# The first modulation sums on quarters of the PSUM rows, and a fixed TensorE order at the start of a DeltaNet/gMLP block

## The chip, the cores and the metric

The kernel runs on one core of a Trainium2 chip. The metric is the time of one execution on the device, in microseconds (us), as the median of several runs. A core has a matrix engine (TensorE, PE in the rows; PEld are its weight loads), VectorE (DVE), ScalarE (ACT), GpSimd (POOL) and a sync engine (SP) that issues nearly all DMA transfers here. Each engine takes its own instructions strictly in order and waits where an operand is not there yet.

## The reference

One step of a hybrid backbone, one layer, over 128 context rows and 2048 latent rows of width 1024:

- modulation: `m = silu(cond) @ w_mod + b_mod` for two conditioning vectors (context and latent), six vectors of 1024 each: shift, scale and gate for the mixer and for the MLP
- `h = rmsnorm(x, norm_mix) * (1 + scale1) + shift1`
- one combined projection of `h`: query, key and value (a centred convolution of width 3 and silu follow), a gate, 16 columns for decay and beta ("ab"), and the two inputs of a spatial gating unit
- a gated DeltaNet scan in both directions, 4 heads of 128, and the spatial gating, then one output projection, residual
- the second modulated rmsnorm, a squared-ReLU MLP of width 4096, residual, final rmsnorm

The change touches only the start: the first four half-vectors of the modulation (`shift1` and `scale1`, each in two halves of 512), and the normalised, modulated and projected first block of rows.

## The kernel before

Everything is float32. A product of full precision is three matmuls of rounded parts: each operand is split into a high part (`H`, rounded) and a low part (`L`, the rest), and `mm3` (L220, L221, L222) adds H x H, L x H and H x L in one PSUM bank. A weight tile of 128x512 is split by `split_w`: ScalarE rounds (L191), VectorE subtracts (L192).

The 17 row tiles of 128 go in blocks of three; block 0 holds the context tile and two latent tiles. For a block, `column(k)` makes one of eight column tiles: for block 0 TensorE transposes the three normalised row tiles (L482) into a bank `pt`, ScalarE applies scale and shift per partition (L484, `full`), VectorE makes `kH` (L487) and `kL` (L488). `feature_tile` computes one head of key (gi 1), query (gi 0) or value (gi 2): per column tile one `mm3` with N = 388, eight in all, then `convolve` (ScalarE L534, VectorE L537, L541). Its bank comes from `pj` (three buffers), for the key head 2 of block 0 from `pt` (three buffers). `ab_block` multiplies the 16 ab columns (L609, L610; bank `pm`, two buffers).

The first modulation vectors are made on TensorE directly in float32: `mod_load` fetches eight 128x512 tiles of `w_mod`, and `mod_columns` multiplies them by the conditioning (`scond`, 128x2 per tile, L335) into the rows 0 and 1 of a `pm` bank, copies the 2x512 result (L337, `mrow`) and transposes it to columns (L340); VectorE adds the bias (L343) and, for the scale, multiplies by the norm weight (L347). This is done four times: `m0` (shift, first half), `m1` (scale, first half), `m2` and `m3` (second halves). Column tiles 0 to 3 need the first halves only, 4 to 7 the second. Ten halo rows `xh` (neighbours of the blocks for the convolution) are normalised and modulated apart (`hal`, L387 to L411).

The later modulation vectors come out of `mods`, a list of steps that the loop over heads spreads over its slots: `MOD_STEPS[n]` steps with head tile n of block 0. The first eight (`split_mod_steps`, L359, L360) run on TensorE, the others on VectorE. The order on each engine is made by a scheduler with a timeline of its own from the order of the code; the kernel's code can add ordering constraints. `wp` is a pool of 49 buffers of 128x512 in which weights and their parts rotate.

Of the kernel before, what the change touches and what calls it, by code (L numbers as in the profile page):

```python
# [18 lines left out]
P = 128  # L19
D = 1024  # L20
# [21 lines left out]
MOD_STEPS = (1, 1, 0, 0, 0, 1, 0, 2, 0, 1, 1, 2)  # L42
# [13 lines left out]
AHEAD = 3  # L56
COMPUTE = (mybir.EngineType.DVE, mybir.EngineType.Activation, mybir.EngineType.Pool)
# [5 lines left out]
def hybrid_step(  # L63
# [62 lines left out]
    def make_masks():  # L126
# [3 lines left out]
        bd = {}  # L130
        for w in (2, 4, 8, 16, 32, 64):
# [7 lines left out]
            bd[w] = m  # L139
        for w in (2, 4, 8, 16, 32):  # L140
            V.tensor_tensor(out=om[w], in0=bd[2 * w], in1=bd[w], op=ALU.subtract)
# [45 lines left out]
    def split_w(raw, pool=None, tag="w"):  # L187

        h = (pool or wp).tile([P, 512], F32R, tag=tag, name="wH")
        lo = (pool or wp).tile([P, 512], F32R, tag=tag, name="wL")  # L190
        A.copy(h, raw)  # L191
        V.tensor_tensor(out=lo, in0=raw, in1=f32(h), op=ALU.subtract)  # L192
        return h, lo
# [87 lines left out]
    with ExitStack() as ph:  # L281
# [29 lines left out]

        def norm_rows(dst):
# [18 lines left out]
        def mod_columns(raws, half, dst, bias, scaled):  # L331

            pm = pm1()
            for k in range(KT):
                T.matmul(pm[0:2, :], scond[:, k, :], raws[k], start=k == 0, stop=k == KT - 1)  # L335
            row = p1.tile([2, 512], F32, tag="mrow", name="mrow", bufs=1)
            A.copy(row, pm[0:2, :])  # L337
            pc = pm1()
            for i in range(4):
                T.transpose(pc[:, 2 * i : 2 * i + 2], row[:, i * P : (i + 1) * P], ident[0:2, 0:2])  # L340
# [4 lines left out]
            if scaled:  # L345
                for cd in range(2):
                    V.scalar_tensor_tensor(out=dst[:, cd, ks], in0=dst[:, cd, ks], scalar=1.0,  # L347
                                           in1=vec[:, 16 + half * 4 : 20 + half * 4], op0=ALU.add, op1=ALU.mult)
# [20 lines left out]

        m0 = mod_load(0, 0)  # L370
        load(out=vec, in_=v_columns)
        convw = vec[:, 32:68].rearrange("p (w a) -> p w a", w=3)
        m1 = mod_load(0, D)
        mod_columns(m0, 0, b1, vec[:, 0:8], False)


        xh = p1.tile([P, D], F32, tag="x", name="xh", bufs=3)[0:10, :]
        for m in range(5):
            r0 = 255 + 384 * m
            load(out=xh[2 * m : 2 * m + 2, :], in_=x_sample[0, r0 : r0 + 2, :])  # L380
# [3 lines left out]
        halL = p1.tile([P, 12 * KT], F32R, tag="halL", name="halL", bufs=1)[:, : 10 * KT].rearrange("p (k j) -> p k j", k=KT)  # L384
        ps = pt()
        for k in range(KT):
            T.transpose(ps[:, k * 10 : k * 10 + 10], xh[:, k * P : (k + 1) * P], ident[:10, :10])  # L387
        V.tensor_copy(hal, ps[:, 0:80].rearrange("p (k j) -> p k j", k=KT))
        xs0 = []
        for t in BLOCKS[0]:  # L390
            x = p1.tile([P, D], F32, tag="x", name="x", bufs=3)
            load(out=x, in_=xrow(t))
            xs0.append(x)
        for x in xs0:
            norm_rows(x)
# [9 lines left out]
        def first_half(half):  # L405
            for k in range(half * 4, half * 4 + 4):
                V.tensor_scalar(out=hal[:, k, :], in0=hal[:, k, :], scalar1=a1[:, 1, k : k + 1],
                                scalar2=b1[:, 1, k : k + 1], op0=ALU.mult, op1=ALU.add)
            ks = slice(half * 4, half * 4 + 4)
            V.tensor_copy(halH[:, ks, :], hal[:, ks, :])  # L410
            V.tensor_tensor(out=halL[:, ks, :], in0=hal[:, ks, :], in1=f32(halH)[:, ks, :], op=ALU.subtract)  # L411

        def prep_block(bi):
# [49 lines left out]
            if bi == 0:  # L463
                zc, hc = [0, 129, 130], [(387, 1)]
            elif bi == 5:
                zc, hc = [n + 1], [(0, 8)]
            else:
                hc = [(0, 2 * bi - 2), (n + 1, 2 * bi + 1)]
            def column(k):
                full = p1.tile([P, 384], F32, tag="full", name="full", bufs=2)  # L470
                kH = p1.tile([P, 416], F32R, tag="h", name="kH", bufs=24)
                kL = p1.tile([P, 416], F32R, tag="h", name="kL", bufs=24)
                for col in zc:
# [255 lines left out]
        for st in xs_:  # L729
            st()  # L730
# [1376 lines left out]
```

## Time and profile before

| what | value |
|---|---|
| median of three runs | 2567.62 us (2565.78 to 2569.37) |
| profiled execution | 2568.22 us |
| its span, first to last instruction | 2566.1 us |
| TensorE busy | 2535.4 us, 99% of the span |
| mean granted TensorE clock | 0.999 |
| VectorE / ScalarE / GpSimd busy | 1771.7 / 1212.2 / 315.1 us |
| HBM traffic | 225 GB/s over the span |

The profile is one execution. A row of the time line gives start (us), length (us), engine, line, operation, written and read names, how many, and in brackets how long the engine sat idle before it and who released it. A matmul in plain float32 (not rounded) leaves two weight loads and two matmul records. Ends of matmuls are modelled, so two neighbours overlap on paper; the distance of starts is the better measure. A row of a window table gives the window, its length, and per engine busy us and number of instructions, then granted clock, DMA share and GB/s. A row of a group gives busy us and the mean of one in ns, then the idle time before.

### The profile page before, as it was taken

What the parts mean: (1) busy time and instruction counts of PE and PEld (TensorE: products, weight loads), DVE (VectorE), ACT (ScalarE), POOL (GpSimd) and SP (SyncE); (2) the same over time, 40 slices, a digit from 0 to 9 for tenths busy, and PEclk for the clock granted to TensorE, in tenths of its full rate; (3) what the DMA queues carried; (4) which work ended last, traced back from release to release, by engine and by line L of the source; (5) the groups of instructions that cost most, each with busy time, mean ns of one, the idle gap of its engine ahead of it and who ended that gap; (6) DMA issues with size and microseconds to landing.
All of it is one profiled execution on the core that took longest, in us unless ns stands there. A gap on an engine that the chain in (4) does not pass through costs nothing.

```text
span 2566.1 us, 43746 instructions
## 1 busy us (share of the span) xinstructions
PE 2535.4 (99%) x15296; PEld 2131.9 (83%) x15296; DVE 1771.7 (69%) x3491; ACT 1212.2 (47%) x2792; POOL 315.1 (12%) x512
## 2 busy tenths in 40 slices
PE   8999999999999999999999999999999999999998
PEld 4899999788888788888888888888888888888887
DVE  5777746667667778885687786776675545685874
ACT  4755545554545567863356553333243333243441
POOL 3112112222222233431000000000000000000000
PEclk9999999999999999999999999999999999999999
DMA  8866637755555758995777797454599878686772
GB/s 295 287 229 204 193 124 222 246 162 170 173 169 177 227 189 271 290 307 200 279 228 235 227 296 265 143 155 142 181 310 316 272 256 305 230 263 208 241 259 91
DMA packets 533858, 579.76 MB, mean 226 GB/s; under 512 B 35500, under 2 KB 366684, under 8 KB 530054
## 3 DMA queue, kind: packets, MB, share of 16 engines
q1 hardware_dynamic: 533638, 576.98, 69.4%
q8 instruction: 120, 1.97, 0.3%
q14 instruction: 100, 0.82, 0.1%
HBM read 397.62 MB, written 179.22 MB: 225 GB/s over the span
## 4 chain that ended last, share of the span: by engine, by line
PE 74%; DVE 2%; DMA 1%; ACT 1%; issue 1%; POOL 0%; SPq 0%; DVEq 0%; POOLq 0%; ACTq 0%
PE f L220 17%; PE f L221 17%; PE f L222 17%; PE pj L220 3%; PE pj L222 3%; PE pj L221 3%; PE pd L994 2%; PE pm L220 1%; PE pm L222 1%; PE pm L221 1%; PE pd L1098 1%; PE pd L1099 1%; PE pd L1062 1%; PE pd L1189 1%; PE pd L1195 1%
## 5 line engine op out<-in xcount | busy, mean ns | idle before, releaser
L220 PE MATMUL f<-hop,zH 128*128 128x512 f32 x960 | 373.2, 389 | 0.0
L222 PE MATMUL f<-hop,zL 128*128 128x512 f32 x960 | 373.1, 389 | 0.0
L221 PE MATMUL f<-hop,zH 128*128 128x512 f32 x960 | 373.1, 389 | 0.0
L220 PE MATMUL f<-hop,wH 128*128 128x512 f32 x896 | 351.6, 393 | 0.3 <-ACT x L1677 0.3
L221 PE MATMUL f<-hop,wH 128*128 128x512 f32 x896 | 349.1, 390 | 0.0
L222 PE MATMUL f<-hop,wL 128*128 128x512 f32 x896 | 344.2, 390 | 0.0
L1601 ACT CAST zH<-zraw 128x512 fp32r<-128x512 f32 x240 | 146.5, 620 | 287.7 <-DMA zraw<-s_d 97.3
L1595 DVE TENSOR_TENSOR zL<-zraw,zH 128x512 fp32r<-128x512 f32 x240 | 162.8, 689 | 75.4 <-ACT zH L1601 63.6
L220 PEld LDWEIGHTS f<-hop,zH 128*128 128x128 f32 x960 | 180.2, 188 | 37.4
L222 PEld LDWEIGHTS f<-hop,zL 128*128 128x128 f32 x960 | 180.2, 188 | 37.4
L221 PEld LDWEIGHTS f<-hop,zH 128*128 128x128 f32 x960 | 180.2, 188 | 37.4
L222 PEld LDWEIGHTS f<-hop,wL 128*128 128x128 f32 x896 | 168.2, 188 | 35.7
L220 PEld LDWEIGHTS f<-hop,wH 128*128 128x128 f32 x896 | 168.5, 188 | 34.7 <-issue 1.2
L221 PEld LDWEIGHTS f<-hop,wH 128*128 128x128 f32 x896 | 168.5, 188 | 32.2
L178 POOL TENSOR_TENSOR r<-rsq,nhalf 128x1 f32<-128x1 f32 (+1 forms) x38 | 25.2, 663 | 1349.1 <-DVE rsq L177 1268.8
L222 PE MATMUL pj<-kH,wL 128*128 128x386 f32 (+2 forms) x568 | 190.5, 335 | 0.0
L220 PE MATMUL pj<-kH,wH 128*128 128x386 f32 (+2 forms) x568 | 189.1, 335 | 0.3 <-DVE kH L487 0.3
L221 PE MATMUL pj<-kL,wH 128*128 128x386 f32 (+2 forms) x568 | 189.3, 333 | 0.0
L1748 ACT CAST wH<-s 128x512 fp32r<-128x512 f32 x96 | 58.9, 620 | 164.1 <-DVE s L1595 149.6
L537 DVE SCALAR_TENSOR_TENSOR cv<-pj,vec,cv 128x384 f32<-128x384 f32 (+2 forms) x164 | 87.4, 541 | 59.8 <-ACT cv L534 58.4
L220 PEld LDWEIGHTS pj<-kH,wH 128*128 128x128 f32 x568 | 107.0, 189 | 4.6 <-issue 4.2
L221 PEld LDWEIGHTS pj<-kL,wH 128*128 128x128 f32 x568 | 107.4, 189 | 0.5
(409 smaller groups left out, 5738.1 us busy)
## 6 DMA issues: line engine op xcount, KB each, us to landing
zraw<-z_d SPq DMA_DIRECT2D x212, 256.0 KB
raw<-in_w_ff_dram SPq DMA_DIRECT2D x128, 256.0 KB
hop<-hop_d SPq DMA_DIRECT2D x28, 1024.0 KB
z_d<-c SPq DMA_DIRECT2D x96, 256.0 KB
zraw<-s_d SPq DMA_DIRECT2D x96, 256.0 KB
raw<-in_w_mod_dram SPq DMA_DIRECT2D x80, 256.0 KB
r<-in_w_ff_dram SPq DMA_DIRECT2D x80, 256.0 KB
s_d<-s SPq DMA_DIRECT2D x64, 256.0 KB
```

The lines of the kernel that those rows point to most:

```text
L220: T.matmul(ps, lh, rh, start=first and i == 0, stop=False, skip_group_check=more)
L221: T.matmul(ps, lh, rl, start=False, stop=False, skip_group_check=more)
L222: T.matmul(ps, ll, rh, start=False, stop=last and i == n - 1, skip_group_check=more)
L537: V.scalar_tensor_tensor(out=cv[:, o : o + m], in0=ps[:, s + sh : s + sh + m], scalar=convw[:, w, j : j + 1], in1=cv[:, o : o + m], op0=AL ...
L994: T.matmul(p[:, h, :], lhs[:, h, :], rhs[:, h, :], start=True, stop=True)
L1062: pe = first_pe(lambda: [T.matmul(p[:, h, :], u["T"][:, h, :], u["vt"][:, h, :], start=True, stop=True) for h in reversed(range(H))])
L1098: T.matmul(p[:, h, :], u["qT"][:, h, :], s[:, h, :], start=True, stop=False)
L1099: T.matmul(p[:, h, :], u["QK"][:, h, :], u["vn"][:, h, :], start=s is None, stop=True)
L1189: T.matmul(py[:, h], g["X"][:, h, :], pm[:, h], start=True, stop=True)
L1595: V.tensor_tensor(out=out, in0=a, in1=b, op=op)
L1601: A.copy(h, src)
L1748: A.copy(h, s2)
```

## The change

It has these parts, all in the first part of the kernel:

- **Sums on quarters.** The conditioning is padded to 32 columns (`sc32`), and matmul k of a sum writes the 32 PSUM rows from 32 x (k mod 4): four partial sums on four quarters, two matmuls each. The whole 128x512 bank is copied, and instead of transposing, a matmul with `sel` (four stacked 32-column identities) adds the quarters while it turns them into columns.
- **A fixed TensorE order.** `in_row` makes each TensorE instruction of a piece follow the last one of the piece before; `behind_row` does the like, as an ordering hint, for the weight splits on the other engines.
- **Piece by piece.** Four key heads instead of three start together. For each of the column tiles 0 to 3: the column's transposes, the four heads' products, then half of a second-half sum (`m2` in tiles 0 and 1, `m3` in 2 and 3). Then half of the ab products, the last columns, tiles 4 and 5, and the rest as before. Twelve matmuls (`WARM`) stand behind the second columns; nothing reads their result.
- **Loads.** The three row tiles and the first four key weights are loaded ahead of `m2` and `m3`; the halo rows are issued from ScalarE's queue.
- **Smaller edits.** The low parts of the query weights are made on GpSimd; the halo column of block 0 comes from an added one-column matmul, so ScalarE and VectorE work on 257 columns at once; halo rows are modulated in one piece; `MOD_STEPS` gives no step to the first five head tiles; the mask building is split and placed earlier.

```diff
-MOD_STEPS = (1, 1, 0, 0, 0, 1, 0, 2, 0, 1, 1, 2)
+MOD_STEPS = (0, 0, 0, 0, 0, 1, 1, 2, 1, 1, 1, 2)
+WARM = 12
...
+        def in_row(fn):
+
+            start = len(tc.nc.cur_bb.bb.instructions)
+            fn()
+            made = [x for x in tc.nc.cur_bb.bb.instructions[start:] if x.engine == mybir.EngineType.PE]
+            for x in made:
+                if row_end:
+                    tc.add_manual_dep(x, row_end[-1].name, mybir.DependencyInfo(
+                        mybir.DependencyClass.NoSync, mybir.DependencyReason.DATA), reason="order")
+            row_end.append(made[-1])
...
-            for k in range(KT):
-                T.matmul(pm[0:2, :], scond[:, k, :], raws[k], start=k == 0, stop=k == KT - 1)
-            row = p1.tile([2, 512], F32, tag="mrow", name="mrow", bufs=1)
-            A.copy(row, pm[0:2, :])
+            def part(k0, k1):
+                for k in range(k0, k1):
+                    j = 32 * (k % 4)
+                    T.matmul(pm[j : j + 32, :], sc32[:, k, :], raws[k], start=k < 4, stop=k >= 4)
...
+            row = p1.tile([P, 512], F32, tag="mrow", name="mrow", bufs=1)
+            A.copy(row, pm)
             pc = pm1()
-            for i in range(4):
-                T.transpose(pc[:, 2 * i : 2 * i + 2], row[:, i * P : (i + 1) * P], ident[0:2, 0:2])
+            def columns():
+                for i in range(4):
+                    T.matmul(pc[:, 2 * i : 2 * i + 2], row[:, i * P : (i + 1) * P], sel[:, 0:2], start=True, stop=True)
+            in_row(columns)
...
+        pm, part = mod_products(m1)
+        in_row(lambda: part(0, KT))
+        mod_columns(pm, 0, a1, bias1, vec[:, 16:24])
+        ps = pt()
+        in_row(lambda: [T.matmul(ps[:, 0:P], ones, mcum[0], start=True, stop=True) for _ in range(WARM)])
...
+                    T.matmul(ps[:, 3 * P : 3 * P + 1], xh[:, k * P : (k + 1) * P], ident[:10, 1:2], start=True, stop=True)
...
-        us = [feature_tile(blk, 0, 1, h) for h in range(3)]
+        us = [feature_tile(blk, 0, 1, h) for h in range(4)]
+        ab1, ab2 = ab_block(blk, 0)
         for k in range(4):
-            cols[k]()
-            for u in us:
-                u["main"][k]()
-        mod_columns(m2, 1, b1, vec[:, 0:8], False)
-        mod_columns(m3, 1, a1, vec[:, 8:16], True)
+            in_row(cols[k])
+            in_row(lambda: [u["main"][k]() for u in us])
...
+            if k % 2 == 0:
+                pm, part = mod_products((m2, m3)[k // 2])
+            in_row(lambda: part(k % 2 * 4, k % 2 * 4 + 4))
+            if k == 1:
+                mod_columns(pm, 1, b1, vec[:, 0:8])
+        W1[1] += [behind_row(lambda: split_w(r)) for r in wk]
+        in_row(lambda: ab1(0, 4))
+        mod_columns(pm, 1, a1, bias1, vec[:, 16:24])
+        for k in (4, 5):
+            in_row(cols[k])
+            in_row(lambda: [u["main"][k]() for u in us])
+        cols[6]()
+        cols[7]()
+        W1[0] += [behind_row(lambda: split_w(r, low=G)) for r in wq[:4]]
```

Lines of the changed kernel: L373 is the sum, L380 its copy, L385 the columns, L444 the twelve matmuls, L531 and L532 the column's transposes and the added matmul, L223 to L225 the three matmuls of `mm3`, L664 and L665 ab, L588 the convolution on VectorE, L404 and L405 the modulation steps on TensorE.

How this moves instructions shows at three places. The first is the start of TensorE's program (a row is line, operation, written and read names, shape). Before:

```order
L335 MATMUL pm<-raw,scond 2x512 x8
L340 MATMUL pm<-ident,mrow 128x2 x4
L335 MATMUL pm<-raw,scond 2x512 x8
L387 MATMUL pt<-ident,xh 128x10 x8
L482 MATMUL pt<-ident,x 128x128 x2
L340 MATMUL pm<-ident,mrow 128x2 x4
L335 MATMUL pm<-raw,scond 2x512 x8
L340 MATMUL pm<-ident,mrow 128x2 x4
L335 MATMUL pm<-raw,scond 2x512 x8
L482 MATMUL pt<-ident,x 128x128
L340 MATMUL pm<-ident,mrow 128x2 x4
```

The same place with the change:

```order
L373 MATMUL pm<-raw,sc_248 32x512 x8
L385 MATMUL pm<-sel,mrow 128x2 x4
L432 MATMUL pt<-ident,xh 128x10 x8
L373 MATMUL pm<-raw,sc_248 32x512 x8
L385 MATMUL pm<-sel,mrow 128x2 x4
L444 MATMUL pt<-mcum_237,ones 128x128 x12
L531 MATMUL pt<-ident,x 128x128 x3
L532 MATMUL pt<-ident,xh 128x1
L223 MATMUL pj<-kH,wH 128x388 x2
```

Two of the four sums now stand ahead of the first head product (L223), the other two behind it. The second place is the change-over from one column tile to the next on TensorE. Before, with three heads:

```order
L221 MATMUL pt<-kL,wH 128x388
L222 MATMUL pt<-kH,wL 128x388
L610 MATMUL pm<-kL,abW 128x388
L482 MATMUL pt<-ident,x 128x128 x3
L220 MATMUL pj<-kH,wH 128x388 x2
L220 MATMUL pt<-kH,wH 128x388
L609 MATMUL pm<-kH,abW 128x388
L482 MATMUL pt<-ident,x 128x128 x3
```

With the change, from the first tile to the second:

```order
L224 MATMUL pj<-kL,wH 128x388
L225 MATMUL pj<-kH,wL 128x388
L373 MATMUL pm<-raw,sc_248 32x512 x4
L531 MATMUL pt<-ident,x 128x128 x3
L532 MATMUL pt<-ident,xh 128x1
L223 MATMUL pj<-kH,wH 128x388 x2
```

Before, the transposes between two tiles belong to later columns (six stand ahead of the first low products); now a column's own transposes stand directly ahead of its products, behind half a sum. The third place is the end of the key heads, with buffer numbers. Before:

```order
L222 MATMUL pj_495<-kH_739,wL_654 128x388
L220 MATMUL pt_499<-kH_739,wH_653 128x388
L221 MATMUL pt_499<-kL_740,wH_653 128x388
L222 MATMUL pt_499<-kH_739,wL_654 128x388
L220 MATMUL pj_993<-kH_467,wH_791 128x388
```

With the change:

```order
L225 MATMUL pj_496<-kH_794,wL_682 128x388
L665 MATMUL pm_685<-kL_795,abW_256 128x388
L224 MATMUL pj_500<-kL_795,wH_681 128x388
L225 MATMUL pj_500<-kH_794,wL_682 128x388
L224 MATMUL pt_504<-kL_795,wH_681 128x388
L225 MATMUL pt_504<-kH_794,wL_682 128x388
L224 MATMUL pj_508<-kL_795,wH_681 128x388
L225 MATMUL pj_508<-kH_794,wL_682 128x388
L223 MATMUL pj_1044<-kH_475,wH_815 128x388
```

The query head (pj_993, now pj_1044) took the third `pj` buffer before; now the key heads hold three (pj_496, pj_500, pj_508), and it follows in the first of them.

More of the change, by code (lines that the diff above doesn't have):

```diff
@@ L185, in raw_w, with split_w @@
         return t
[L187 removed]
+    def split_w(raw, pool=None, tag="w", low=V):
         h = (pool or wp).tile([P, 512], F32R, tag=tag, name="wH")
@@ L191, in split_w @@
         A.copy(h, raw)
-        V.tensor_tensor(out=lo, in0=raw, in1=f32(h), op=ALU.subtract)
+        low.tensor_tensor(out=lo, in0=raw, in1=f32(h), op=ALU.subtract)
         return h, lo
@@ L310, in hybrid_step, with behind_row @@
         V.tensor_scalar_mul(scond.rearrange("p k c -> p c k"), st_.rearrange("p (c k) -> p c k", c=2), 0.5)
+        sc32 = p1.tile([P, KT, 32], F32, tag="sc32", name="sc32", bufs=1)
+        V.memset(sc32, 0.0)
+        V.tensor_copy(sc32[:, :, 0:2], scond)
+        sel = p1.tile([P, 64], F32, tag="sel", name="sel", bufs=1)
+        bias1 = sel[:, 32:40]
+        V.tensor_copy(sel[:, 0:32], ident[:, 0:32])
+        for j in range(1, 4):
+            V.tensor_tensor(out=sel[:, 0:32], in0=sel[:, 0:32], in1=ident[:, 32 * j : 32 * j + 32], op=ALU.add)
+        row_end = []
+        def in_row(fn):
[7 more added lines that the diff above has]
+            row_end.append(made[-1])
+        def behind_row(fn):
+            start = len(tc.nc.cur_bb.bb.instructions)
+            got = fn()
+            for x in tc.nc.cur_bb.bb.instructions[start:]:
+                if x.engine in COMPUTE:
+                    tc.add_manual_dep(x, row_end[-1].name, mybir.DependencyInfo(
+                        mybir.DependencyClass.NoSync, mybir.DependencyReason.DATA), reason="order")
+            return got
         def norm_rows(dst):
@@ L344, in mod_columns @@
                             in1=bias[:, ks].unsqueeze(1).to_broadcast([P, 2, 4]), op=ALU.add)
[L345 to L348, printed above, removed]
+            if weight is not None:
+                V.tensor_tensor(out=d, in0=d, in1=weight[:, ks].unsqueeze(1).to_broadcast([P, 2, 4]), op=ALU.mult)
         def split_mod_steps(jc):
@@ L372, in hybrid_step @@
         convw = vec[:, 32:68].rearrange("p (w a) -> p w a", w=3)
+        V.tensor_scalar_add(bias1, vec[:, 8:16], 1.0)
         m1 = mod_load(0, D)
[L374 to L380, printed above, removed]
         norm_rows(xh)
@@ L403, in hybrid_step, with halo_rows @@
         W1 = {0: [], 1: [], 2: []}
[L405 to L411, printed above, removed]
+        def halo_rows():
+            for tab, op in ((a1, ALU.mult), (b1, ALU.add)):
+                V.tensor_tensor(out=hal, in0=hal, in1=tab[:, 1, :].unsqueeze(2).to_broadcast([P, KT, 10]), op=op)
+            V.tensor_copy(halH, hal)
+            V.tensor_tensor(out=halL, in0=hal, in1=f32(halH), op=ALU.subtract)
         def prep_block(bi):
@@ L730, in hybrid_step @@
             st()
+        wr = load_w1(1, range(4))
+        abr = p1.tile([P, KT, 16], F32, tag="abr", name="abr", bufs=1)
+        load(out=abr, in_=w_ab)
         m2 = mod_load(1, 0)
         m3 = mod_load(1, D)
[L733 to L738 removed]
+        W1[1] += [split_w(r) for r in wr[:2]]
```

88 lines of the change are left out of this document (51 added, 37 removed).

## The prediction

> **What bounds the kernel now.** I read the page first, then the busy time by stage, then the instructions in order of time over the first 60 us, and last the waits.
>
> ```profile
> span 2566.1 us, 43746 instructions
> PE 2535.4 (99%) x15296; PEld 2131.9 (83%) x15296; DVE 1771.7 (69%) x3491; ACT 1212.2 (47%) x2792; POOL 315.1 (12%) x512
> ...
> 0.00:4.00 4.00, 0.00 (x0) 0.00 (x1) 1.97 (x12) 1.50 (x2) 3.27 (x21) 1.00 0.41 130
> 4.00:40.70 36.70, 33.91 (x93) 7.88 (x94) 10.19 (x35) 11.09 (x20) 9.46 (x64) 1.00 1.01 360
> 40.70:80.00 39.30, 39.30 (x236) 38.50 (x236) 34.17 (x98) 29.13 (x80) 11.69 (x23) 1.00 0.77 254
> 80.00:100.00 20.00, 17.06 (x105) 15.44 (x103) 15.69 (x36) 12.30 (x39) 0.85 (x1) 1.00 0.74 223
> 100.00:220.00 120.00, 119.65 (x715) 113.29 (x716) 89.42 (x172) 68.14 (x211) 26.03 (x74) 1.00 0.69 223
> ```
>
> TensorE is busy 99% of the span, and from 40.7 us on it has work all the time except in 80 to 100. Everything the change touches lies before about 220 us; behind that, TensorE's program is the same row for row. So the change is worth what it moves the moment at which TensorE has a given amount of block 0 behind it. Up to 40.7 us TensorE is also "busy" (33.91 of 36.70), but with what?
>
> ```profile
> 4.03 9.41 PE L335 MATMUL pm<-raw,scond 128*2 128x512 f32 x16 [4.03 <-DMA raw<-in_w_mod_dram]
> 14.19 0.38 PE L340 MATMUL pm<-ident,mrow 2*128 2x2 f32 x4 [0.76 <-ACT mrow L337]
> 14.50 7.03 PE L335 MATMUL pm<-raw,scond 128*2 128x512 f32 x16
> 21.46 0.66 PE L387 MATMUL pt<-ident,xh 10*128 10x10 f32 x8
> ...
> 23.49 7.03 PE L335 MATMUL pm<-raw,scond 128*2 128x512 f32 x16
> 31.24 0.41 PE L340 MATMUL pm<-ident,mrow 2*128 2x2 f32 x4 [0.72 <-ACT mrow L337]
> 31.57 7.03 PE L335 MATMUL pm<-raw,scond 128*2 128x512 f32 x16
> 38.53 0.33 PE L482 MATMUL pt<-ident,x 128*128 128x128 f32 x1
> ...
> 39.66 0.50 PE L359 MATMUL pm<-wH,abW 128*128 128x512 f32 x1
> 39.99 0.40 PE L360 MATMUL pm<-wL,abW 128*128 128x512 f32 x1
> 40.70 0.59 PE L220 MATMUL pj<-kH,wH 128*128 128x388 f32 x2 [0.32 <-DVE kH L487]
> ...
> 42.14 0.34 PE L221 MATMUL pj<-kL,wH 128*128 128x388 f32 x1
> ...
> 43.37 0.49 PE L482 MATMUL pt<-ident,x 128*128 128x128 f32 x3
> 43.62 0.60 PE L220 MATMUL pj<-kH,wH 128*128 128x388 f32 x2
> ```
>
> Four vector sums (L335: 9.41 and three of 7.03 us) fill it, one behind the other; the first head product (L220) starts at 40.70. From these rows come two prices. Seven products lie between 42.14 and 43.37: 0.176 us each. Three transposes take 43.62 - 43.37 = 0.25, so 0.083 each. A sum is 16 records for 8 matmuls, two passes each, in program order: 7.03/16 = 0.44 us per pass.
>
> **The yardstick.** Let E be the moment at which four key heads over eight column tiles (4 x 8 x 3 = 96 products), the gate projection (16) and the columns' transposes are done. Before, counted as plain work from 40.70: 112 x 0.176 + 21 x 0.083 = 21.5, E = 62.2 us (three transposes were done earlier).
>
> **When the head products start now.** DMA: 16 tiles of 256 KB and three x of 512 KB are 5.8 MB; 0.5 MB land by 4 us (130 GB/s), the rest at 360 GB/s: the third x is there at 18.7 us. The sums decide, because on ScalarE the copy of the second sum stands ahead of the three squares of x. What two passes on different quarters of the PSUM rows cost, no row of before shows: all L335 passes write the same two rows. Bounds for four matmuls (eight passes): 0.9 us if all quarters run at once (one matmul's two passes), 8 x 0.43 = 3.44 if nothing overlaps. I take the case between. The two passes of one matmul stand next to each other and need the same quarter, so the second must follow the first by 0.43 as in these rows, and the next quarter's first pass can start with it at the earliest, as records start in program order. Four matmuls then take 5 x 0.43 = 2.15, eight 9 x 0.43 = 3.9.
>
> ```profile
> 4.83 0.13 PEld L335 LDWEIGHTS pm<-raw,scond 128*2 128x2 f32 x1 [0.72 <-DMA raw<-in_w_mod_dram]
> 5.69 0.13 PEld L335 LDWEIGHTS pm<-raw,scond 128*2 128x2 f32 x1 [0.72 <-issue]
> ...
> 8.98 0.09 PEld L335 LDWEIGHTS pm<-raw,scond 128*2 128x2 f32 x1 [0.61 <-issue]
> 9.41 0.09 PEld L335 LDWEIGHTS pm<-raw,scond 128*2 128x2 f32 x1 [0.34 <-issue]
> ```
>
> The Trainium skill, "TensorE: Matmul & The Clock Gate", section "Part 3: Packing small matmuls — row/col tiling", states that matmuls whose outputs lie on different 32-partition quarters run in the array at once, about 4 ns apart, and gives 2.38x measured for three such tiles. By it four would take about 0.9 us here instead of my 2.15; no run of this case shows it yet, and it is rival 1 below.
>
> The first passes are 0.86 apart, later 0.43 (rows above). So the first sum ends at 10.7 (one step past 8.98 for each of the last four matmuls). Its copy (L337) takes 0.57.
>
> ```profile
> L337 ACT COPY mrow<-pm 2x512 f32<-2x512 f32 x4 | 2.3, 575 | 22.1 <-PE pm L335 22.1
> L340 PEld LDWEIGHTS pm<-ident,mrow 2*128 2x128 f32 x16 | 1.3, 136 | 4.1 <-ACT mrow L337 2.3 <-issue 1.7
> 20.08 1.06 ACT L318 ACTIVATE junk<-x 128x1024 bf16<-128x1024 f32 x1 [1.20 <-DMA x<-in_x_sample_dram]
> 21.04 0.19 ACT L318 ACTIVATION_READ_ACCUMULATOR junk<-x 128x1 f32 x1
> ...
> 22.89 0.33 PE L482 MATMUL pt<-ident,x 128*128 128x128 f32 x1 [0.52 <-DVE x L320]
> ```
>
> The columns are real matmuls now instead of transposes, two passes each, so I count 8 weight loads of 0.136 = 1.1 us. Copy and columns bring 12.4, the halo rows' transposes (0.66, L387) 13.1, the second sum 17.0, its copy 17.7, three squares of 1.15 each (1.06 + 0.19, overlapping by 0.1) 21.15. From the end of a square to the transpose that reads the normed x it takes 22.89 - 21.23 = 1.66: 22.8. The twelve added 128x128 matmuls behind the second columns (24 passes at 0.14, a weight load each: 3.4 us, 18.9 to 22.3) fit in this wait and cost nothing; were they longer they would be late for the same transposes.
>
> Then the column chain, which returns at every tile: transposes, ScalarE scales two pieces, VectorE rounds, TensorE multiplies.
>
> ```profile
> 39.17 0.90 ACT L484 ACTIVATE full<-pt,b,a 128x128 f32<-128x128 f32 x2
> 40.27 0.28 DVE L487 CAST kH<-full 128x256 fp32r<-128x256 f32 x1
> ```
>
> Three transposes and the added one-column matmul (two passes with a weight load of 0.14 each) 0.53, their end 0.25 later, 0.90, 0.28, some 0.05 at the hand-overs: 2.0 us. First product at 24.8.
>
> **The first half, piece by piece.** The fixed order puts each column's transposes directly ahead of its own products, behind the sum pieces; before, the transposes stood several tiles ahead and the chain was hidden under products. So the chain is paid openly. Blocks: 4 x 12 x 0.176 = 8.4. Sum pieces: 4 x 2.15 = 8.6. Chains of tiles 1 to 3: 6.0. Columns behind the second piece: copy 0.57 with 0.2 of hand-over, 1.1 of matmuls: 1.85. Half the gates: 8 x 0.176 = 1.4; the last sum's copy lies beside it. Last columns 1.1, then 0.6 for two small VectorE operations and hand-overs, and 0.90 + 0.28 + 0.15 for the fifth tile, whose transposes lie beside: 3.05. Together 24.8 + 8.4 + 8.6 + 6.0 + 1.85 + 1.4 + 3.05 = 54.1 us. The data is not late: the last tile for the fourth sum comes at 4 + (11.1 - 0.5)/0.36 = 33.4 us.
>
> **The second half.** 56 x 0.176 = 9.9, nine transposes 0.75, three more one-column matmuls 0.84, a rest of 0.25 of the sixth tile's chain: 65.8. Next comes the first query head. Four key heads now hold all three pj banks and one pt, where before three heads left one pj free; the query head's first product waits until VectorE has read the first key head's bank.
>
> ```profile
> 58.42 0.60 DVE L612 COPY absb<-pm 32x128 f32<-32x128 f32 x2
> 58.96 2.41 DVE L537 SCALAR_TENSOR_TENSOR cv<-pj,vec,cv 128x128 f32<-128x128 f32 x7
> ...
> L1051 POOL TENSOR_TENSOR se<-S,egl 128x512 f32<-128x512 f32 x30 | 35.1, 1169 | 131.6 <-DVE S L1087 105.6 <-DMA S<-in_state_delta_dram 20.2 <-DVE rsq L177 5.7
> ```
>
> That bank is full 1.2 us (seven products) ahead of E; the gate copy (0.60) and five of the convolution's operations (2.41/7 = 0.34 each) come first: 1.05 - 0.17 - 0.60 - 1.72 = -1.5, a wait of 1.5 us. Two matmuls of the gate-modulation step (L359, L360; about 0.2 each) that lay ahead of 40.70 come later: 0.4. The low parts of the query weights move from VectorE to GpSimd, at 1.17 instead of 0.69 us: eight end at about 60.1 + 9.4 = 69.5, and TensorE needs the eighth at 67.3 + 7 x 0.53 = 71.0. Hidden; without that cover up to 2 us. The single-piece halo rows, merged columns of zeros and the halo loads on ScalarE's queue lie off TensorE's path.
>
> E with these: 65.8 + 1.5 + 0.4 = 67.7, against 62.2: **5.5 us later**.
>
> **What comes back.** In 80 to 100 us TensorE waits for modulation steps:
>
> ```profile
> PE pm L359 <- ACT wH L191: 2.6, 2, 1.9
> ...
> 78.84 0.33 SPq L184 DMA_DIRECT2D raw<-in_w_mod_dram x1
> ...
> 84.45 0.62 ACT L191 CAST wH<-raw 128x512 fp32r<-128x512 f32 x1 [2.96 <-DMA raw<-in_w_mod_dram]
> 85.12 0.50 PE L359 MATMUL pm<-wH,abW 128*128 128x512 f32 x1 [1.90 <-ACT wH L191]
> ```
>
> A tile issued at 78.84 was used at 84.45. The change lets these steps begin with the sixth head tile, and the first two of their tiles are issued directly behind the value weights. Bounds: nothing comes back, or all 2.6 us. I take the long wait, 1.9. Result: 5.5 - 1.9 = +3.6 on the profiled execution of 2568.2, which is 0.6 above the median shown (2567.6): **2571 us**, +0.14%, within the 0.2% that a measurement of this kernel cannot tell from no change.
>
> **Rivals.** 1. All quarters run at once. The pieces cost 4 x 0.9 instead of 4 x 2.15 (-5.0), the second sum ends with its data (15.9 instead of 17.0, -1.2): 2565; with the bank wait and the other 0.7 of the modulation waits gone too, 2563. Against it speaks the order of the two passes in the rows.
> 2. The quarters do not overlap, so the change does not do what it says. The first sum ends at 13.4 as before, the second at 22.9, first product at 30.7 (+5.9); the pieces cost 4 x 1.29 more (+5.2): 2582, slower. For it speaks that the only rows with this operand are strictly 0.43 apart; it decides as soon as four matmuls of a piece take over 2.6 us.
> 3. The clock. The first passes of the run were twice as long. If TensorE idles long enough between the twelve matmuls and the first block to fall back, that block and its sum piece (2.1 + 2.15) double: 2575.
> 4. The chain is shorter than 2.0, since ScalarE's and VectorE's pieces overlap more: 0.4 less on four tiles, 2569.
>
> **Chances.** Forecast, with rival 4: 0.45 (its own range 2566 to 2576); rival 1: 0.28; rival 2: 0.17; rival 3: 0.10. Faster by over 0.2% (below 2562.5) needs rival 1 and more: 0.16, and 0.01 of the forecast: 0.17. Slower (above 2572.8): all of rival 2, 0.07 of rival 3, 0.14 of the forecast: 0.38. Within: 0.45. Range 2561 to 2583: it takes in both ends of the sums.
>
> **What would show it.** In the changed profile: L373's passes, four matmuls in 0.9, 2.15 or 3.4 us; the first L223 at 24.8; before each L223 block an idle of about 1.5 us with VectorE's kH as releaser, and one of 0.8 before the columns with ScalarE's mrow; the first product of the query head idle for 1.5 behind VectorE's cv; no long L404 wait around 85. I am wrong if TensorE's idle between 25 and 54 us sums to under 3 us.

## The result and the profile after

The changed kernel takes **2582.48 us** (median; 2581.5 to 2584.08) beside 2566.7 us for the kernel before on the same chip: a ratio of 1.0058, 95% interval 1.0046 to 1.007, so 0.58% slower. That is half a microsecond inside the range of the prediction, but far above its forecast of 2571 and outside the forecast's own range of 2566 to 2576. (Ratios and their intervals are those on record; the quotient of the two medians differs from them by up to 0.0006.) Which steps held and which did not is what the rest is about.

The page of the changed kernel's profiled execution:

```profile
span 2582.3 us, 43840 instructions
PE 2539.4 (98%) x15352; PEld 2144.4 (83%) x15352; DVE 1767.7 (68%) x3480; ACT 1211.9 (47%) x2792; POOL 319.5 (12%) x488
```

The span is 16.2 us longer. TensorE's instructions in order of time, from the second sum to the modulation steps (start, length, line, names, shape, count, and in brackets the idle time before and who ended it):

```profile
13.71 4.03 PE L373 MATMUL pm<-raw,sc 128*32 128x512 f32 x16
...
26.37 0.62 PE L223 MATMUL pj<-kH,wH 128*128 128x388 f32 x2 [1.57 <-DVE kH L538]
26.83 0.34 PE L223 MATMUL pt<-kH,wH 128*128 128x388 f32 x1
27.01 0.33 PE L223 MATMUL pj<-kH,wH 128*128 128x388 f32 x1
27.18 0.45 PE L224 MATMUL pj<-kL,wH 128*128 128x388 f32 x1
27.43 0.53 PE L225 MATMUL pj<-kH,wL 128*128 128x388 f32 x1
27.75 0.53 PE L224 MATMUL pj<-kL,wH 128*128 128x388 f32 x1
...
29.82 1.46 PE L373 MATMUL pm<-raw,sc 128*32 128x512 f32 x8
31.22 0.55 PE L531 MATMUL pt<-ident,x 128*128 128x128 f32 x3
...
33.51 0.59 PE L223 MATMUL pj<-kH,wH 128*128 128x388 f32 x2 [1.44 <-DVE kH L538]
...
60.02 0.59 PE L223 MATMUL pj<-kH,wH 128*128 128x388 f32 x2 [1.64 <-DVE kH L538]
...
75.69 0.41 PE L223 MATMUL pj<-kH,wH 128*128 128x388 f32 x1 [1.60 <-DVE cv L588]
...
87.59 0.52 PE L600 MATMUL pt<-ident,x 128*128 128x128 f32 x3 [2.08 <-DVE x L592]
89.17 0.79 PE L404 MATMUL pm<-wH,abW 128*128 128x512 f32 x1 [1.06 <-ACT wH L194]
```

The rhythm is the one foretold: half a sum, transposes, a wait for VectorE's `kH`, twelve products. But from 27.4 us on the products start 0.32 us apart, not 0.176 as at 26.83 and 27.01. The same engine's windows, cut at 3.41 us (window, length, busy us and instructions of PE, PEld, DVE, ACT, POOL, granted TensorE clock, DMA share, GB/s), say why:

```profile
20.48:23.90 3.42, 2.27 (x19) 1.84 (x17) 2.23 (x7) 2.35 (x6) 1.11 (x2) 1.00 1.07 382
23.90:27.31 3.41, 1.57 (x8) 1.37 (x9) 3.34 (x10) 1.42 (x3) 0.00 (x0) 0.99 1.05 386
27.31:30.72 3.41, 3.41 (x17) 2.27 (x15) 0.21 (x2) 0.00 (x0) 3.12 (x8) 0.51 1.05 386
30.72:34.14 3.42, 1.98 (x17) 1.27 (x10) 1.47 (x5) 1.42 (x3) 1.61 (x5) 0.99 1.06 388
34.14:37.55 3.41, 3.41 (x14) 2.78 (x16) 0.29 (x1) 0.00 (x0) 0.00 (x0) 0.51 1.07 391
37.55:40.96 3.41, 2.57 (x21) 1.49 (x13) 0.17 (x1) 0.59 (x1) 0.00 (x0) 0.99 1.04 378
40.96:44.38 3.42, 1.99 (x6) 2.02 (x7) 1.15 (x4) 0.92 (x2) 0.00 (x0) 0.50 0.86 295
44.38:47.79 3.41, 3.41 (x15) 1.92 (x14) 0.00 (x0) 0.00 (x0) 0.00 (x0) 0.51 0.81 255
47.79:51.20 3.41, 1.93 (x13) 1.39 (x10) 1.59 (x5) 2.15 (x5) 0.00 (x0) 0.99 0.67 194
51.20:54.62 3.42, 3.42 (x14) 2.53 (x16) 1.97 (x4) 0.83 (x2) 0.00 (x0) 0.51 0.30 100
```

The granted clock is either full or half, and it changes only at these cuts. In this profile a window in which TensorE waits for the chain (busy 1.57, 1.98, 2.57, 1.93 of 3.41 us) is followed by one at half clock, and in that window the block of products falls. So each block pays twice: for the wait, and for the slow clock that the wait brings. Between 25 and 65 us six such windows are at half clock (the sixth, from 61.4 us, is not shown); the kernel before had none there.

### The profile page after: what moved, and what is told of

Its sections match the earlier page's. It is cut to its first block, busy times and chain, and to the rows that moved or that the text cites. A ratio compares the mean times of both kernels' runs of the same rounds, so it can differ in the third digit from the quotient of the medians.

```text
span 2582.3 us, 43840 instructions
## 1 busy us (share of the span) xinstructions
PE 2539.4 (98%) x15352; PEld 2144.4 (83%) x15352; DVE 1767.7 (68%) x3480; ACT 1211.9 (47%) x2792; POOL 319.5 (12%) x488
## 3 DMA queue, kind: packets, MB, share of 16 engines
q8 instruction: 121, 1.98, 0.3%
## 4 chain that ended last, share of the span: by engine, by line
PE 59%; DVE 3%; DMA 1%; ACT 1%; issue 1%; SPq 0%; POOL 0%; DVEq 0%; POOLq 0%; ACTq 0%
PE f L223 17%; PE f L224 17%; PE f L225 17%; PE pj L223 1%; PE pj L225 1%; PE pj L224 1%; PE pd L1066 1%; DMA x<-in_x_sample_dram 0%; PE pd L1170 0%; PE pd L1171 0%; PE pm L223 0%; PE pm L225 0%; PE pm L224 0%; PE pd L1134 0%; PE pm L1487 0%
## 5 line engine op out<-in xcount | busy, mean ns | idle before, releaser
L223 PE MATMUL f<-hop,zH 128*128 128x512 f32 x960 | 373.2, 389 | 0.0
L225 PE MATMUL f<-hop,zL 128*128 128x512 f32 x960 | 373.1, 389 | 0.0
L223 PE MATMUL f<-hop,wH 128*128 128x512 f32 x896 | 351.6, 393 | 0.3 <-ACT x L1749 0.3
L225 PE MATMUL f<-hop,wL 128*128 128x512 f32 x896 | 344.2, 390 | 0.0
L225 PEld LDWEIGHTS f<-hop,zL 128*128 128x128 f32 x960 | 180.2, 188 | 37.4
L223 PEld LDWEIGHTS f<-hop,zH 128*128 128x128 f32 x960 | 180.2, 188 | 37.4
L223 PE MATMUL pj<-kH,wH 128*128 128x386 f32 (+2 forms) x568 | 191.0, 339 | 9.6 <-DVE kH L538 7.6
L225 PEld LDWEIGHTS f<-hop,wL 128*128 128x128 f32 x896 | 168.2, 188 | 35.8
L223 PEld LDWEIGHTS f<-hop,wH 128*128 128x128 f32 x896 | 168.5, 188 | 34.9 <-issue 1.2
L225 PE MATMUL pj<-kH,wL 128*128 128x386 f32 (+2 forms) x568 | 193.2, 341 | 0.0
L588 DVE SCALAR_TENSOR_TENSOR cv<-pj,vec,cv 128x384 f32<-128x384 f32 (+2 forms) x164 | 87.3, 539 | 58.1 <-ACT cv L585 56.6
L223 PEld LDWEIGHTS pj<-kH,wH 128*128 128x128 f32 x568 | 107.6, 190 | 14.8 <-issue 10.3
```

The source lines that it names most:

```text
L223: T.matmul(ps, lh, rh, start=first and i == 0, stop=False, skip_group_check=more)
L225: T.matmul(ps, ll, rh, start=False, stop=last and i == n - 1, skip_group_check=more)
L588: V.scalar_tensor_tensor(out=cv[:, o : o + m], in0=ps[:, s + sh : s + sh + m], scalar=convw[:, w, j : j + 1], in1=cv[:, o : o + m], op0=AL ...
```

## Experiments

Theory A, formed on this profile: the sums on quarters do what they should; the loss is the open chain of transposes, scaling and rounding at every column tile, and the half clock that its waits bring. Theory B: the products are slow for another reason (DMA traffic, or the switch between quarter and full matmuls), and the waits are only what was foretold. All ratios are to the kernel before on the same chip.

| kernel | median, us | ratio (95%) |
|---|---|---|
| changed | 2582.48 | 1.0058 (1.0046 to 1.007) |
| changed, measured again | 2587.51 | 1.0073 (1.0059 to 1.0086) |
| waits filled with idle matmuls | 2577.87 | 1.0028 (1.0017 to 1.0039) |
| transposes one tile ahead | 2570.30 | 1.0004 (0.9995 to 1.0013) |
| before, only its sums on quarters | 2576.03 | 1.0024 (1.0014 to 1.0034) |
| changed, sums on two rows | 2594.16 | 1.0093 (1.0077 to 1.011) |
| changed, order left free | 2574.41 | 1.0017 (1.0008 to 1.0026) |
| ahead, three heads | 2565.49 | 0.9983 (0.9974 to 0.9992) |
| ahead, five idle matmuls | 2569.93 | 1.0003 (0.9994 to 1.0012) |
| ahead, three heads, five idle matmuls | 2563.89 | 0.9976 (0.9967 to 0.9984) |
| the last with the old `MOD_STEPS` | 2566.96 | 0.9994 (0.9985 to 1.0003) |
| changed, three heads | 2577.45 | 1.0035 (1.0022 to 1.0047) |
| changed, one warming matmul | 2587.43 | 1.0071 (1.0059 to 1.0084) |

**Fill the waits.** `fill` issues n matmuls like the twelve of `WARM`, which nothing reads.

```diff
             in_row(cols[k])
+            fill(7)
             in_row(lambda: [u["main"][k]() for u in us])
```

> The changed kernel with seven more idle-time matmuls (128x128, float32, the same as the twelve after the second columns, result unused) between each of the first five columns' transposes and its products; nothing else is moved. They take about 7 x 0.24 = 1.7 us, the length of the wait that they fill. Theory A (the clock): the waits leave TensorE half idle, the granted clock falls to 0.59 to 0.84, and a product costs 0.32 us instead of 0.176; then the filled waits bring the clock back to 1.0, five blocks of products fall from 3.2 to 4.2 us each to about 2.1, E from 74 to about 67 us and the time from 2582 to about 2575. Rival (the products are slow because of the saturated DMA or of the switch between 32-row and 128-row writes): product distance stays 0.32, time 2582 to 2584.

Measured: ratio 1.0028 (2577.87 us, where about 2575 was expected). TensorE of this kernel from the first block to the second (L448 are the idle matmuls, L536 the transposes):

```profile
26.82 0.62 PE L223 MATMUL pj<-kH,wH 128*128 128x388 f32 x2
...
29.10 1.06 PE L373 MATMUL pm<-raw,sc 128*32 128x512 f32 x8
30.10 0.55 PE L536 MATMUL pt<-ident,x 128*128 128x128 f32 x3
...
30.88 1.83 PE L448 MATMUL pt<-mcum,ones 128*128 128x128 f32 x14
32.56 0.59 PE L223 MATMUL pj<-kH,wH 128*128 128x388 f32 x2
```

Between 17.5 and 82 us the clock is never at half, the block takes 2.28 us (26.82 to 29.10) instead of 3.45, and half a sum 1.0 instead of 1.4. From first product to first query head it is 41.07 us instead of 49.32. The chain itself is as long as before (2.46 us from the transposes at 30.10 to the products, 2.29 in the changed kernel). DMA share (1.05) and the switch to quarters are as in the changed kernel, so theory B falls. Work that does nothing gained 0.3% (0.45% against the second measurement of the changed kernel), since it stood where TensorE would have waited anyway.

**Transposes one tile ahead.** Nothing added or removed; column k+1's transposes stand ahead of column k's products.

```diff
-            in_row(cols[k])
+            if k == 0:
+                in_row(cols[0])
+            if k < 3:
+                in_row(cols[k + 1])
             in_row(lambda: [u["main"][k]() for u in us])
...
-        for k in (4, 5):
-            in_row(cols[k])
-            in_row(lambda: [u["main"][k]() for u in us])
+        in_row(cols[4])
+        in_row(cols[5])
+        in_row(lambda: [u["main"][4]() for u in us])
+        in_row(lambda: [u["main"][5]() for u in us])
```

> The changed kernel with the transposes of the next column tile ahead of this tile's products (tiles 1 to 3, and tile 5 ahead of tile 4's products); no instruction is added. The chain transposes - ScalarE - VectorE then lies under products and a sum piece. Theory A (waits, and the clock as their consequence): the idle of 1.4 to 1.6 us ahead of four blocks goes (about -6), the clock stays up (about -6 more): 2570. Rival (only the waits cost, the slow products have another cause): -6 alone, 2576. Rival (the fixed order is not what costs): 2582.

Measured: 1.0004 and 2570.30 us, the kernel before again, and what theory A had. What is left of TensorE's waits between the first product and 100 us in this kernel:

```profile
25.76 1.02 PE L223 MATMUL pj<-kH,wH 128*128 128x388 f32 x2 [0.79 <-DVE kH L538]
...
61.39 0.41 PE L223 MATMUL pj<-kH,wH 128*128 128x388 f32 x1 [1.84 <-DVE cv L588]
72.20 0.52 PE L600 MATMUL pt<-ident,x 128*128 128x128 f32 x3 [0.99 <-DVE x L592]
...
25.41:28.82 3.41, 3.06 (x9) 3.06 (x10) 2.35 (x9) 1.04 (x3) 0.96 (x2) 0.50 1.06 388
```

The last row is its only half-clock window between the first product and 100 us; waits of 0.78 us ahead of the columns and of 0.2 us ahead of transposes are left out. One wait for `kH` instead of five, one half-clock window instead of six, and the first query head 14.3 us earlier. The loss of the change sits in the place of four columns' transposes in TensorE's order.

**Only the quarters.** The kernel before with its sums, their copy and their columns as in the change, and no other edit.

```diff
-                T.matmul(pm[0:2, :], scond[:, k, :], raws[k], start=k == 0, stop=k == KT - 1)
+                j = 32 * (k % 4)
+                T.matmul(pm[j : j + 32, :], sc32[:, k, :], raws[k], start=k < 4, stop=k >= 4)
```

> The kernel before with only the sums changed: 32 columns on four quarters of the PSUM rows, the whole bank copied, columns by matmuls with the stacked identities; order of code, loads and heads as before. In the changed kernel eight passes on quarters took 1.2 to 1.6 us instead of 3.44. If the four sums (7.03 us each) set the first head product at 40.7 us, it comes about 6 us earlier (then bound by the 11.1 MB that land by about 33 us, a copy and a column chain): 2560 to 2562. If the start was bound by DMA or the third row tile in any case: 2566, no change. Theory A predicts no slow products here, since the transposes stand ahead.

Measured: 1.0024, slower than before: both expectations missed. The first product did move, from 40.70 to 35.01. The gain was lost behind it. TensorE's waits of this kernel in the first 230 us (engine, line, releaser: us in total, times, longest), then the row with the longest of them and its neighbour, then the two rows of VectorE ahead of it:

```profile
PE pj L220 <- DVE cv L546: 3.5, 2, 3.0
...
PE pm L368 <- ACT wH L191: 2.8, 2, 2.4
PE pj L220 <- ACT wH L191: 1.1, 1, 1.1
PE pj L618 <- DVE cv L546: 0.9, 1, 0.9
```

```profile
131.81 0.66 PE L220 MATMUL pj<-kH,wH 128*128 128x386 f32 x1 [3.02 <-DVE cv L546]
132.27 0.53 PE L221 MATMUL pj<-kL,wH 128*128 128x386 f32 x1
```

```profile
129.72 1.41 DVE L256 SCALAR_TENSOR_TENSOR acc<-raw,scond,acc 128x512 f32<-128x512 f32 x2 [0.40 <-DMA raw<-in_w_mod_dram]
131.05 0.61 DVE L546 SCALAR_TENSOR_TENSOR cv<-pj,vec,cv 128x384 f32<-128x384 f32 x1
```

At 131.81 a head of block 1 waits 3.0 us for a bank. The convolution that frees it (L546) stands on VectorE behind two modulation sums (L256), which had waited 0.40 us for their weights. The clock halves with the wait (from 132.3 us on products start 0.32 us apart). The number of these sums is not the reason: between 116 and 132 us the kernel before has the same twelve (8.4 us of VectorE, here 8.5) and no such wait. The kernel before idles only 0.35 us of TensorE in 100 to 150 us, this one 4.7. The waits listed (8.3 us) and two half-clock windows behind the first product (from 66.9 and from 131.8 us) are the visible part of the loss; how they add up to it was not taken apart.

**The sums on two rows again**, in the changed order: the opposite of the last one.

```diff
-                    j = 32 * (k % 4)
-                    T.matmul(pm[j : j + 32, :], sc32[:, k, :], raws[k], start=k < 4, stop=k >= 4)
+                    T.matmul(pm[0:2, :], scond[:, k, :], raws[k], start=k == 0, stop=k == KT - 1)
```

> The changed kernel with the sums on two rows as before (2 columns, rows 0 and 1, copy of two rows, transposes to columns); order, heads, loads as changed. It prices the quarters in this order: four pieces of about 3.44 instead of 1.4 us (+8) and the first two sums about 3 us later each where data is not the limit (+4 to +6). By theory A TensorE is busier between the blocks, so the clock may fall less and give back up to 6: 2588 to 2596. If the quarters are worth nothing here: 2582.

Measured: 1.0093. Half a sum in this kernel:

```profile
30.93 3.60 PE L372 MATMUL pm<-raw,scond 128*2 128x512 f32 x8
```

3.60 us against 1.06 on quarters at full clock. In the changed order the quarters are worth 0.35% (1.0093 against 1.0058), some 9 us (0.2% or 5 us against the second measurement, 1.0073). The expectation held. Four half sums of 2.5 us each are 10, and the first product comes 2.3 us later (28.64); against that stand three half-clock windows between 25 and 65 us instead of six.

**The order left free.** `in_row` adds no constraint.

```diff
-                if row_end:
-                    tc.add_manual_dep(x, row_end[-1].name, ...)
+                pass
```

> The changed kernel without the fixed TensorE order: in_row adds no constraint, everything else stays. The scheduler now puts the next tile's transposes ahead of the low products of the present tile, and the sums' matmuls partly elsewhere. Theory A (it is the open chain of transposes, scaling and rounding, and the low clock it brings, that costs; the order does so only by putting the transposes directly ahead of their products): the L221 to L223 blocks run at 0.176 per product after the first, waits for kH sum to under 3 us, and the time is that of the version with the transposes moved ahead, 2566 to 2574. Rival (the order as such protects the start; left free, waits arise elsewhere, as in the kernel before with only its sums changed): 2575 or more, with new waits for modulation weights or convolutions after 60 us.

Measured: 1.0017, at the edge between the two. The scheduler put the next transposes among the present products, and no wait for `kH` is left; but it also drew the twelve warming matmuls (`WARM`) into the first sum, where they no longer stand ahead of the transposes. The clock was at half from 21.5 to 31.6 us, and once more from 52.2 us:

```profile
25.56 2.00 PE L371 MATMUL pm<-raw,sc 128*32 128x512 f32 x4
27.49 1.02 PE L223 MATMUL pj<-kH,wH 128*128 128x388 f32 x2
```

The order written in the change costs 0.4% against the scheduler's; the one with the transposes ahead is at least as good as the scheduler's (1.0004, with intervals that overlap). So a fixed order need not cost anything.

**Three key heads, idle matmuls, both**, all on the version with the transposes ahead.

```diff
-        us = [feature_tile(blk, 0, 1, h) for h in range(4)]
+        us = [feature_tile(blk, 0, 1, h) for h in range(3)]
...
+            if k == 0:
+                fill(5)
             in_row(lambda: [u["main"][k]() for u in us])
```

> The version with the transposes one tile ahead, with three key heads at the start instead of four, and the head order of the kernel before (the first query head takes the third pj bank). Theory A: the wait of 1.84 us of the first query head for VectorE's cv goes, and perhaps the 0.99 us for x behind it: 1.8 to 2.8 us faster than with four heads (2570.3 beside 2569.1 of the kernel before), so 2567.5 to 2568.5. Rival (VectorE is what is late, not the bank: the wait returns at a later bank or at a modulation step): no change, about 2570.

> The version with the transposes one tile ahead and four heads, with five idle matmuls between the second tile's transposes and the first product (seven took 1.64 us, so 1.17). Theory A (the first block ran at half clock because TensorE idled 0.27, 1.15 and 0.79 us within 4 us): with the 0.79 filled the block takes 2.28 instead of 3.70; the start is 0.4 later: 1.0 faster, 2569.3. Rival (the earlier 1.15 alone brings the clock down): the block stays at 3.7 and the time is 0.4 longer, 2570.7.

> Transposes ahead, three key heads and the five idle matmuls together. Theory A: the two gains add, 2.8 to 3.8 us below the version with transposes ahead: 2566.5 to 2567.5, which is 1.5 to 2.5 us (0.06 to 0.1%) below the kernel before, if that is 2569. Rival: VectorE's backlog takes both back, 2569 to 2570.

Measured: 0.9983, 1.0003 and 0.9976. Three heads gain more than expected (0.21% against the version with four, some 5 us). The waits for cv and x are gone; the first query head starts without any (a row without brackets):

```profile
59.06 0.41 PE L223 MATMUL pj<-kH,wH 128*128 128x388 f32 x1
```

A wait of 1.32 us for ScalarE's `wH` (at 70.99) is new. Besides, its first block happened to run at full clock without any filling, which the version with four heads had not. The five idle matmuls alone change nothing measurable (1.0003 and 1.0004). They did hold the clock over the first block, and in that profile a later window was halved instead, behind waits that left the clock alone in the version without them:

```profile
27.43:30.84 3.41, 3.41 (x23) 2.16 (x23) 1.27 (x4) 0.00 (x0) 2.03 (x5) 1.00 1.05 387
...
34.26:37.67 3.41, 2.63 (x21) 2.29 (x18) 0.32 (x2) 1.22 (x3) 0.00 (x0) 1.00 1.05 384
37.67:41.08 3.41, 3.41 (x17) 2.24 (x16) 3.34 (x8) 2.56 (x5) 0.00 (x0) 0.54 1.04 374
```

All three together are the fastest version here, 0.24% below the kernel before (0.16 to 0.33%), at 2563.89 us. Whether the idle matmuls add anything to the three heads is not settled: the intervals 0.9974 to 0.9992 and 0.9967 to 0.9984 overlap.

**The old `MOD_STEPS`** in that fastest version.

```diff
-MOD_STEPS = (0, 0, 0, 0, 0, 1, 1, 2, 1, 1, 1, 2)
+MOD_STEPS = (1, 1, 0, 0, 0, 1, 0, 2, 0, 1, 1, 2)
```

> The version with transposes ahead, three key heads and five idle matmuls, with the MOD_STEPS of the kernel before (one step each with the first two head tiles, as it was). Theory A (the modulation steps are hidden in either place once TensorE no longer waits at the start): the same as with the new numbers within 0.1%, 0.9976 of the kernel before, about 2564. Rival (early steps put ScalarE's and VectorE's work ahead of the convolutions): 2 us or more slower than that.

Measured: 0.9994; the gain is all but gone. One wait of TensorE stands out that the fastest version does not have; the rows under it are VectorE's ahead of its end:

```profile
117.56 0.41 PE L224 MATMUL pj<-kL,wH 128*128 128x386 f32 x1 [3.23 <-DVE kL L553]
...
116.00 0.88 DVE L257 TENSOR_SCALAR acc<-raw,scond 128x512 f32<-128x512 f32 x2 [3.35 <-DMA raw<-in_w_mod_dram]
116.79 0.62 DVE L553 SCALAR_TENSOR_TENSOR kL<-full,b,kH 128x384 fp32r<-128x384 f32 x1
```

VectorE had no backlog here: it stood still for 3.35 us, because the next instruction in its order was a modulation sum (L257) whose weights had not come, and the `kL` that TensorE needs stands behind that sum. A half-clock window follows (from 117.9 us). In the kernel with only the quarters a convolution stood behind such sums in the same way. So the later steps are a real part of the change's worth, though not at the place where the prediction looked for it. The quarters with the later steps alone, in the order of the kernel before, were not run.

**Three heads, and one warming matmul, in the changed kernel itself.**

> The changed kernel with three key heads at the start instead of four, everything else as changed (fixed order, transposes directly ahead of their products). Theory A: the 1.6 us that the first query head waited for VectorE's cv go, and 24 products move from the slow start (up to 0.32 each) to the full clock behind it, which is worth up to 24 x 0.14 = 3.4 us: 2 to 5 us faster than the changed kernel, 2577.5 to 2580.5 beside 2582.5. Rival (with nine products per tile instead of twelve TensorE idles a larger share of each tile, so more stretches run at half clock, and this takes the gain back): no faster, 2582 or more.

> The changed kernel with one idle matmul behind the second columns instead of twelve. Theory A (they fill a wait for x and hold the clock up to about 24 us only; the clock falls at 27 us either way, in the wait ahead of the first product): the time stays within 0.1%, 2580 to 2585, the first product stays at about 26.4. Rival (they hold the clock over the start): the transposes and the first block run at half clock from about 24 us, 1 to 2 us slower, 2584 or more.

The edits are the first two lines of the diff above (with the head order of the kernel before, and `n < 3` for `n < 4` in the loop over heads, in all versions with three heads), and `WARM = 1`. Measured: 1.0035 and 1.0071. Three heads gain 0.23% here too, as theory A had it, though five windows between 26 and 61 us are still at half clock. One warming matmul in place of twelve: the clock halves at 19.6 us already, yet the first product stands at 26.07, and the time (1.0071) lies between the two measurements of the changed kernel (1.0058 and 1.0073), though above the 2580 to 2585 expected. The rival was right about the half clock of the first block. In this profile the first query head even comes at 70.06, since only one more window up to 100 us is at half clock; behind 100 us TensorE idles more instead (100 to 150 us: 2.5 us, 0.9 in the changed kernel). So no worth of the twelve matmuls can be measured; they end at 22.3, ahead of the waits that matter.

**The changed kernel again.**

> The changed kernel once more, unaltered, for a second profile of it. Half clock came in stretches of 3.41 us that begin on a grid of that step (27.3, 34.1, 41.0, 51.2, 61.4 us, one of them double). Theory A (the grid runs on by itself and lies elsewhere in each execution, and which waits fall into one of its cells decides): other stretches are slow this time, but again five or more of them between 25 and 70 us, 16 to 21 us at half clock in all, and the time is again 2580 to 2585, 1.0046 to 1.007 of the kernel before. Rival (the first profile was an unlucky one): under 10 us at half clock, and a median nearer to 2575; then the clock is no full explanation of the loss.

Measured: 1.0073. Half-clock windows began at 27.7, 34.5 and 58.1 us only, three between 25 and 65 us, not six:

```profile
27.38 0.76 PE L223 MATMUL pj<-kH,wH 128*128 128x388 f32 x2 [1.57 <-DVE kH L538]
...
72.76 0.41 PE L223 MATMUL pj<-kH,wH 128*128 128x388 f32 x1 [1.60 <-DVE cv L588]
...
34.51:37.92 3.41, 3.39 (x11) 3.41 (x12) 0.94 (x2) 0.04 (x1) 0.00 (x0) 0.50 1.06 389
37.92:41.34 3.42, 2.64 (x21) 1.48 (x20) 0.03 (x1) 0.59 (x1) 0.00 (x0) 1.00 1.05 384
41.34:44.75 3.41, 1.93 (x12) 1.70 (x11) 1.29 (x5) 0.92 (x2) 0.00 (x0) 1.00 0.94 332
```

The waits are the same to 0.1 us, the clock is not. From first product to first query head it is 45.4 us here, 49.3 in the first profile, 41.1 with the waits filled: 4.3 us for three windows and 8.2 for six, 1.4 us for each. The two profiled executions took 2580.67 and 2584.08 us. The five executions of this measurement order themselves in the same way: those at a mean granted clock of 0.996 took 2580.4 and 2580.7 us, those at 0.992 took 2589.3 and 2590.1. A window of 3.41 us at half clock lowers the mean over 2582 us by 0.0007, so 0.004 are some six windows for 9 us, 1.5 us each by this estimate. The expectation of five or more windows missed, and the median of 2587.51 us lies above the 2580 to 2585 expected.

The loads, the low parts on GpSimd and the edits of the halo rows were not tested apart.

## Why the prediction was right or wrong

By its own steps, with the changed kernel's first profile:

| step | predicted | measured |
|---|---|---|
| second sum ends, us | 17.0 | 17.74 |
| first product, us | 24.8 | 26.37 |
| four half sums | 8.6 | 5.4 |
| **four blocks of twelve products** | **8.4** | **14.8** |
| chains of tiles 1 to 3 | 6.0 | 6.9 |
| columns behind the second piece | 1.85 | 1.7 |
| half the gates | 1.4 | 1.5 |
| last columns and the fifth chain | 3.05 | 3.3 |
| second half with the bank wait | 13.2 | 15.7 |
| first query head, us | 67.3 | 75.7 |
| waits in 80 to 100 us that come back | 1.9 | 0 |

That the time fell inside the range is luck. The upper end of 2583 was drawn for rival 2, in which the quarters do not overlap, and they do; measured again, the changed kernel took 2587.51 us, outside the range.

- **The step that failed is the price of the blocks**: 12 x 0.176, taken from rows in which TensorE never waited. Rival 3 had the right mechanism and put it in the wrong place: one block and one piece behind the twelve matmuls, +4. It came behind every open chain. Filling the waits took 7.8 us off the first query head and 0.3% (some 8 us, and 4 more or less by the intervals) off the time, so this term is shown, not argued.
- **The chain** was right in kind and a little short: 2.3 us from transposes to product against 2.0, with waits of 1.44 to 1.64 for VectorE's `kH` ahead of each block. TensorE's idle between 25 and 54 us is over 3 us, so the condition under which the prediction called itself wrong did not occur.
- **The quarters** do more than the forecast granted: four matmuls in 1.06 us at full clock, next to the lower bound of 0.9, not the 2.15 that the order of the two passes had suggested. Rival 1's price for the half sums was right, its earlier end of the second sum was not: that sum took 4.03 us, where the prediction had 3.9, and ended at 17.74. The Trainium skill, "TensorE: Matmul & The Clock Gate", section "Part 3: Packing small matmuls — row/col tiling", has matmuls on different quarters run at once; the trace agrees, for two-pass float32 matmuls too.
- **The bank wait** was foretold as 1.5 us and is 1.60, with the releaser foretold. Taking the fourth key head away gained 5 to 6 us in both orders (in the order of the change nearly 10 against its second measurement), more than this wait; where the rest comes from in the faster of the two was not taken apart beyond the wait for x (0.99) and a first block at full clock (1.4).
- **The modulation waits** did not come back. The wait at 89.17 is 1.06 instead of 1.9, but one of 2.08 for VectorE's `x` stands ahead of it (87.59), which no step had; together 3.1 us, as long as TensorE's idle there before (2.9). VectorE is late there with the convolutions of four key heads at once: with three heads and the transposes ahead neither row is left. No wait for the low parts made on GpSimd shows up to 230 us, as foretold.
- **The size.** E came 13.9 us late (75.7 plus the 0.4 of the two moved matmuls, less 62.2) where the prediction had 5.5, and nothing came back; of the 16.2 us of the span 2.3 lie behind, among them another half-clock window from 88 us on.

## What to carry to other kernels

When an order is written out by hand, put what the next block needs (here its transposes) ahead of the present block's products: the same instructions one place earlier were worth 0.54%. Price a block of matmuls that stands behind a repeated wait at half clock as well as at full, and look at the granted clock in windows as short as the rhythm of the work, since the page's first slice of 65 us shows only an 8 in place of a 9. A gain at the start is kept only if what feeds the next stage is not overtaken by it. Here that is VectorE's convolutions and the modulation sums among them, which wait for their weights: quarters alone lost (1.0024), and with the transposes ahead, three heads at once and later modulation steps they gained (0.9976).

## What was not expected of the hardware

- Waits of 1.4 to 1.6 us, once per 7 to 10 us, were enough to halve the clock. Full windows were followed by half ones with TensorE busy between 1.57 and 2.63 of 3.41 us (the rows above), while others with 2.27 (20.48 above, mostly warming matmuls) or 1.58 were not, as around the bank wait in the version with transposes ahead:

```profile
59.54:62.96 3.42, 1.58 (x10) 1.60 (x10) 3.42 (x7) 1.36 (x3) 3.42 (x3) 1.00 0.81 225
62.96:66.37 3.41, 3.41 (x23) 3.19 (x21) 2.48 (x4) 2.32 (x5) 0.46 (x1) 1.00 1.01 404
```

  The plainest pair are two windows of the changed kernel, both with 1.93 us busy: half clock followed the one at 47.79 in the first profile, full clock the one at 41.34 in the second. The busy share in the records does not decide alone; what does was not settled.
- Each half-clock stretch is 3.41 us or twice or three times that, on a grid of this step that lies elsewhere in each of these profiles (from 27.31 us in the first, from 27.68 in the second). The Trainium skill, "TensorE: Matmul & The Clock Gate", section "Part 1: The HAM clock gate (the "warmup" mystery)", states a free-running window of 3413 ns and a clock gate with two states, half and full rate; these traces agree with both (3.41 us, 0.50 and 1.00). The same waits cost three windows in one execution and six in another, 2.9 us at the first query head (72.76 and 75.69).
- At half clock the products stand 0.32 us apart, not 0.352, twice 0.176.
